# Rotary embedding on one core: 2 MB transfers, and the adds of ten of 32 tiles on TensorE

## The chip, the cores and the metric

The kernel runs on one core of a Trainium2 chip. The metric is the device time of one execution in microseconds (us); lower is better. The profile of the changed kernel shows the timelines of five engines: TensorE (PE, 160 instructions, and PEld for its 160 weight loads), VectorE (DVE, 61), ScalarE (ACT, 43), GpSimd (POOL, 62) and SyncE (SP), which issues the loads (17). The stores are issued by ScalarE, and the page counts 16 DMA engines that carry the transfers. Waits of one engine for another stand in the trace as semaphore instructions (25 on the line of DVE's adds). The span in a profile is 1.7 to 2.1 us shorter than the device time of the same execution.

## The reference

The input x has 8 × 2048 × 8 × 64 elements of fp32 (33.5 MB), and the output is as large. Each half row of 32 is combined with the other half:

```python
def reference(x, cos, sin):
    x1 = x[..., : x.shape[-1] // 2]
    x2 = x[..., x.shape[-1] // 2 :]
    cos = cos[None, :, None, :]
    sin = sin[None, :, None, :]
    out1 = x1 * cos - x2 * sin
    out2 = x1 * sin + x2 * cos
    return np.concatenate([out1, out2], axis=-1)
```

So every output element is one product with cos, one product with plus or minus sin of the other half, and one add.

## The kernel before

The data are cut into 32 tiles of 128 partitions × 2048 elements, 1 MB each. For a tile, GpSimd makes the two sine products (1024 elements per partition each) into a buffer t2, DVE makes the cosine product into t1 and then adds t1 and t2 into the tile itself, which is stored from there. The buffers: there are three of t2, one of t1 (in PSUM), and twenty tiles of x.

```python
    t1_pool = ctx.enter_context(tc.tile_pool(name="t1p", bufs=1, space=bass.MemoryType.PSUM))
    xpool = ctx.enter_context(tc.tile_pool(name="xpool", bufs=20))
    t2_pool = ctx.enter_context(tc.tile_pool(name="t2p", bufs=3))
    # ... tables of cos and sin ...
    for i, (b, l) in enumerate(tiles):
        xt = xpool.tile([P, FREE], f32, tag="xt", name=f"xt{i}")
        nc.sync.dma_start(out=xt, in_=xv[b, :, l * FREE : (l + 1) * FREE])
        xts.append(xt)
    # ...
    for i, (b, l) in enumerate(tiles):
        xt = xts[i]
        t1 = t1_pool.tile([P, FREE], f32, tag="t1")
        t2 = t2_pool.tile([P, FREE], f32, tag="t2")
        for u in range(2):
            # dst, src: views of the two halves of t2 and of xt (cut)
            nc.gpsimd.tensor_mul(out=dst..., in0=src..., in1=rep(ssin[...], H))      # L73
        nc.vector.tensor_mul(out=t1..., in0=xt..., in1=rep(cos_ps[...], 2 * H))     # L78
        nc.vector.tensor_add(out=xt, in0=t1, in1=t2)                                # L83
        nc.scalar.dma_start(out=ov[b, :, l * FREE : (l + 1) * FREE], in_=xt)
```

## Time and profile before

| | before |
|---|---|
| device time, median of 3 | 168.17 us |
| span of the profiled run | 166.6 us |
| DVE busy | 148.2 us |
| GpSimd busy | 146.3 us |
| bytes moved | 67.65 MB |

These lines are from the page of the kernel before: the span, the busy times, and the 40 slices of the span, in which a digit is a busy share in tenths (9 is 90% or more).

```profile
DVE 148.2 (89%) x67; POOL 146.3 (88%) x68
...
DVE  0169999999999999999999999999999999999980
POOL 0299999999999999999999999999999999998000
DMA  5999999999999999999999999999999999999656
...
DVE 89%; DMA 5%; issue 2%; DVEq 0%; ACTq 0%
...
L73 POOL TENSOR_TENSOR t<-xt,ssin 128x1024 f32<-128x1024 f32 x64 | 146.1, 2341 | 6.8 <-DVE ssin L58 6.8
L83 DVE TENSOR_TENSOR xt<-t,t 128x2048 f32<-128x2048 f32 x32 | 73.3, 2291 | 3.3
L78 DVE TENSOR_TENSOR t<-xt,cos_ps 128x2048 f32<-128x2048 f32 x32 | 73.5, 2296 | 1.1
```

The line that begins "DVE 89%" is the chain of waits, followed back from the last instruction: nearly all of it is DVE. The three groups below it end with "idle before, releaser". GpSimd's 64 products were idle only for the 6.8 us of the start, so GpSimd never waits for a buffer; DVE's adds and products lose next to nothing. Three resources are full together: DVE, GpSimd and, until the last three slices, the DMA engines. Relief of one of them alone can win little: 67.65 MB at the 427 GB/s of the middle (next view) are 158 us without start and end (here and below, GB/s count loads and stores together).

In windows of the span (start and end, then its length, busy time of each engine with the number of instructions, the granted TensorE clock, the DMA share and GB/s), before reads:

```profile
40.00:80.00 40.00, 38.79 (x18) 40.00 (x18) 1.00 1.01 427
130.00:167.00 37.00, 30.88 (x14) 23.36 (x11) 1.00 0.87 364
```

The first busy column is DVE, the second GpSimd. In the middle stage both work nearly all the time *at the same time*.

### The profile page before, as it was taken

Reading aid. Unit: us, or ns where it says so; the run is one execution under the profiler, and the core shown is the slowest. Engines: PE = TensorE matmul, PEld = TensorE weight load, DVE = VectorE, ACT = ScalarE, POOL = GpSimd, SP = SyncE. Lnnn points to the kernel's source line nnn. Section 1 sums busy time; section 2 is a strip of 40 time slices with the busy share of each in tenths; the row PEclk is TensorE's granted clock in tenths of the full one; section 3 lists DMA queues with packets and bytes.
Section 4 is the critical chain, followed back from the end, with each engine's and each line's share of the span. In section 5 each row is a group of like instructions: output and inputs, shape, how many; then the busy total and the mean of one; then the engine's idle time right before and its main releaser. Section 6 shows DMA issues by size and latency. Waiting matters only on the chain.

```text
span 166.6 us, 381 instructions
## 1 busy us (share of the span) xinstructions
DVE 148.2 (89%) x67; POOL 146.3 (88%) x68
## 2 busy tenths in 40 slices
DVE  0169999999999999999999999999999999999980
POOL 0299999999999999999999999999999999998000
DMA  5999999999999999999999999999999999999656
GB/s 167 424 428 421 374 431 423 433 427 425 431 421 431 429 427 427 425 433 419 433 425 423 433 419 433 423 433 427 425 431 421 431 427 427 429 423 433 285 220 252
DMA packets 9506, 67.65 MB, mean 406 GB/s; under 512 B 1056, under 2 KB 1056, under 8 KB 1312
## 3 DMA queue, kind: packets, MB, share of 16 engines
q10 hardware_dynamic: 4896, 34.08, 48.6%
q1 hardware_dynamic: 4608, 33.56, 48.3%
q14 instruction: 2, 0.02, 0.0%
HBM read 34.08 MB, written 33.55 MB: 406 GB/s over the span
## 4 chain that ended last, share of the span: by engine, by line
DVE 89%; DMA 5%; issue 2%; DVEq 0%; ACTq 0%
DVE t L78 44%; DVE xt L83 44%; DMA cos_sb<-in_cos_dram 5%; DVE cos_ps L60 0%; DVEq L83 0%; ACTq L48 0%
## 5 line engine op out<-in xcount | busy, mean ns | idle before, releaser
L73 POOL TENSOR_TENSOR t<-xt,ssin 128x1024 f32<-128x1024 f32 x64 | 146.1, 2341 | 6.8 <-DVE ssin L58 6.8
L83 DVE TENSOR_TENSOR xt<-t,t 128x2048 f32<-128x2048 f32 x32 | 73.3, 2291 | 3.3
L78 DVE TENSOR_TENSOR t<-xt,cos_ps 128x2048 f32<-128x2048 f32 x32 | 73.5, 2296 | 1.1
L58 DVE TENSOR_SCALAR ssin<-sin_sb 128x512 f32<-128x512 f32 x1 | 0.4, 426 | 6.7 <-DMA sin_sb<-in_sin_dram 6.7
L60 DVE COPY cos_ps<-cos_sb 128x512 f32<-128x512 f32 x1 | 0.7, 694 | 2.4 <-DMA cos_sb<-in_cos_dram 2.4
L59 DVE COPY ssin<-sin_sb 128x512 f32<-128x512 f32 x1 | 0.4, 419 | 0.0
L99 POOL MEMSET const-float32-0.0<- 128x1 f32 x1 | 0.1, 98 | 0.2 <-issue 0.2
L99 POOL MEMSET const-bfloat16-1.0<- 128x1 bf16 x1 | 0.1, 101 | 0.0
L99 POOL MEMSET const-uint8-127<- 128x1 uint8 x1 | 0.1, 101 | 0.0
L99 POOL MEMSET const-float32-1.0<- 128x1 f32 x1 | 0.1, 98 | 0.0
## 6 DMA issues: line engine op xcount, KB each, us to landing
xt<-in_x_dram SPq DMA_DIRECT2D x32, 1024.0 KB, 20.6
out_dram<-xt ACTq DMA_DIRECT2D x32, 1024.0 KB, 10.7
sin_sb<-in_sin_dram ACTq DMA_DIRECT2D x1, 256.0 KB, 6.0
cos_sb<-in_cos_dram ACTq DMA_DIRECT2D x1, 256.0 KB, 8.7
```

The costliest lines, as they stand in the source:

```text
L58: nc.vector.tensor_scalar_mul(ssin[:, :, 0, :], sin_sb, -1.0)
L59: nc.vector.tensor_copy(ssin[:, :, 1, :], sin_sb)
L60: nc.vector.tensor_copy(cos_ps, cos_sb)
L73: nc.gpsimd.tensor_mul(out=dst.rearrange("p (r h) d -> p r h d", h=H), in0=src.rearrange("p (r h) d -> p r h d", h=H), in1=rep(ssin[:, l * ...
L78: nc.vector.tensor_mul(out=t1.rearrange("p (r k d) -> p r k d", r=SL, d=Dh), in0=xt.rearrange("p (r k d) -> p r k d", r=SL, d=Dh), in1=rep ...
L83: nc.vector.tensor_add(out=xt, in0=t1, in1=t2)
L99: nc = _bacc.Bacc("TRN2", target_bir_lowering=False, num_devices=1)
```

## The change

The intent is to relieve the two busy engines and to make transfers cheaper. Tiles are loaded and stored in pairs of 2 MB, with rows of 16 KB instead of 8 KB. Twenty-two tiles (kind A) are computed as before. In six tiles (kind B), TensorE adds: a matmul with the identity as weights puts t1 into PSUM, a second one accumulates t2 on top, and ScalarE copies the sum to the tile. In four tiles (kind C), DVE makes both products, GpSimd is left out, and TensorE and ScalarE do the rest. For kinds B and C, t1 lies in SBUF in buffers of its own (t1s, two of them), and t2 gives up one of its three buffers. In the listing, line 118 is the GpSimd product, 123 DVE's cosine product, 129 DVE's add, 111 DVE's sine product of kind C, 134 and 135 the matmuls of kind B with the copy in 136, and 143, 144 and 147 the same of kind C.

```diff
-    xpool = ctx.enter_context(tc.tile_pool(name="xpool", bufs=20))
-    t2_pool = ctx.enter_context(tc.tile_pool(name="t2p", bufs=3))
+    o_pool = ctx.enter_context(tc.tile_pool(name="op", bufs=2, space=PSUM))
+    xpool = ctx.enter_context(tc.tile_pool(name="xpool", bufs=10))
+    t1s_pool = ctx.enter_context(tc.tile_pool(name="t1s", bufs=2))
+    t2_pool = ctx.enter_context(tc.tile_pool(name="t2p", bufs=2))
 ...
+        xt = xpool.tile([P, PAIR], f32, tag="xt", name=f"xt{i}")
+        for lo, n in [(0, FREE), (FREE, FREE)] if i == 0 else [(0, PAIR)]:
+            nc.sync.dma_start(out=xt[:, lo : lo + n], in_=xv[b, :, l * PAIR + lo : l * PAIR + lo + n])
 ...
+    kinds = {3: "C", 11: "C", 18: "C", 24: "C", 6: "B", 9: "B", 14: "B", 16: "B", 21: "B", 27: "B"}
 ...
+        if kind == "A":
+            t1 = t1_pool.tile([P, FREE], f32, tag="t1")
+        else:
+            t1 = t1s_pool.tile([P, FREE], f32, tag="t1s")
 ...
+        if kind == "C":
+            nc.vector.tensor_mul(out=t2..., in0=xk, in1=rep(sin_ps[...], 2 * H))
+        else:
+            # the two GpSimd products, as before
 ...
-        nc.vector.tensor_add(out=xt, in0=t1, in1=t2)
+        if kind == "A":
+            nc.vector.tensor_add(out=xt, in0=t1, in1=t2)
+        elif kind == "B":
+            for j in range(FREE // C):
+                o = o_pool.tile([P, C], f32, tag="o")
+                cs = slice(j * C, (j + 1) * C)
+                nc.tensor.matmul(o, eye, t1[:, cs], start=True, stop=False)
+                nc.tensor.matmul(o, eye, t2[:, cs], start=False, stop=True)
+                nc.scalar.copy(xt[:, cs], o)
+        else:
+            # the same with the halves of t2 swapped, and -identity for one of them
 ...
+        elif half:
+            nc.scalar.dma_start(out=ov[b, :, base : base + PAIR], in_=pt)
```

The last pair is stored as two halves of 1 MB, the first pair loaded as two halves. In SBUF the pools of x are equal before and after (20 × 1 MB, 10 × 2 MB).

More of the change, by code (lines that the diff above doesn't have):

```diff
@@ L20 @@
     f32 = mybir.dt.float32
+    PSUM = bass.MemoryType.PSUM
     B, S, H, D = x.shape
@@ L28 @@
     SL = 4
-    n_blk = R // SL
     FREE = SL * HD
+    PAIR = 2 * FREE
+    n_pair = R // (2 * SL)
+    C = 512
     xv = x.rearrange("b (q r) h d -> b q (r h d)", q=P)
@@ L37 @@
     const_pool = ctx.enter_context(tc.tile_pool(name="const", bufs=1))
-    cps_pool = ctx.enter_context(tc.tile_pool(name="cps", bufs=1, space=bass.MemoryType.PSUM))
-    t1_pool = ctx.enter_context(tc.tile_pool(name="t1p", bufs=1, space=bass.MemoryType.PSUM))
-    xpool = ctx.enter_context(tc.tile_pool(name="xpool", bufs=20))
-    t2_pool = ctx.enter_context(tc.tile_pool(name="t2p", bufs=3))
+    tab_pool = ctx.enter_context(tc.tile_pool(name="tab", bufs=1, space=PSUM))
+    t1_pool = ctx.enter_context(tc.tile_pool(name="t1p", bufs=1, space=PSUM))
+    o_pool = ctx.enter_context(tc.tile_pool(name="op", bufs=2, space=PSUM))
+    xpool = ctx.enter_context(tc.tile_pool(name="xpool", bufs=10))
+    t1s_pool = ctx.enter_context(tc.tile_pool(name="t1s", bufs=2))
+    t2_pool = ctx.enter_context(tc.tile_pool(name="t2p", bufs=2))
     cos_sb = const_pool.tile([P, R, Dh], f32, tag="cb")
@@ L45 @@
     ssin = const_pool.tile([P, R, 2, Dh], f32, tag="ss")
-    cos_ps = cps_pool.tile([P, R, Dh], f32, tag="cp")
+    eye = const_pool.tile([P, P], f32, tag="eye")
+    neye = const_pool.tile([P, P], f32, tag="neye")
+    cos_ps = tab_pool.tile([P, R, Dh], f32, tag="cp")
+    sin_ps = tab_pool.tile([P, R, Dh], f32, tag="sp")
     nc.scalar.dma_start(out=sin_sb, in_=sin_src)
     nc.scalar.dma_start(out=cos_sb, in_=cos_src)
-    tiles = [(b, l) for l in range(n_blk) for b in range(B)]
+    pairs = [(b, l) for l in range(n_pair) for b in range(B)]
     xts = []
-    for i, (b, l) in enumerate(tiles):
-        xt = xpool.tile([P, FREE], f32, tag="xt", name=f"xt{i}")
-        nc.sync.dma_start(out=xt, in_=xv[b, :, l * FREE : (l + 1) * FREE])
-        xts.append(xt)
+    for i, (b, l) in enumerate(pairs):
+        xt = xpool.tile([P, PAIR], f32, tag="xt", name=f"xt{i}")
+        for lo, n in [(0, FREE), (FREE, FREE)] if i == 0 else [(0, PAIR)]:
+            nc.sync.dma_start(
+                out=xt[:, lo : lo + n],
+                in_=xv[b, :, l * PAIR + lo : l * PAIR + lo + n],
+            )
+        xts.append(xt)
+    nc.gpsimd.memset(eye, 0.0)
+    nc.gpsimd.affine_select(
+        out=eye,
+        in_=eye,
+        compare_op=mybir.AluOpType.not_equal,
+        fill=1.0,
+        base=0,
+        pattern=[[-1, P]],
+        channel_multiplier=1,
+    )
     nc.vector.tensor_scalar_mul(ssin[:, :, 0, :], sin_sb, -1.0)
@@ L60 @@
     nc.vector.tensor_copy(cos_ps, cos_sb)
+    nc.scalar.copy(sin_ps, sin_sb)
+    nc.scalar.mul(neye, eye, -1.0)
     def rep(a, n):
         return dataclasses.replace(a, ap=[a.ap[0][:], a.ap[1][:], [0, n], a.ap[-1][:]])
-    for i, (b, l) in enumerate(tiles):
-        xt = xts[i]
-        t1 = t1_pool.tile([P, FREE], f32, tag="t1")
-        t2 = t2_pool.tile([P, FREE], f32, tag="t2")
-        for u in range(2):
-            dst = t2.rearrange("p (rh u d) -> p rh u d", u=2, d=Dh)[:, :, u, :]
-            src = xt.rearrange("p (rh u d) -> p rh u d", u=2, d=Dh)[:, :, 1 - u, :]
-            nc.gpsimd.tensor_mul(
-                out=dst.rearrange("p (r h) d -> p r h d", h=H),
-                in0=src.rearrange("p (r h) d -> p r h d", h=H),
-                in1=rep(ssin[:, l * SL : (l + 1) * SL, u, :], H),
-            )
+    kinds = {3: "C", 11: "C", 18: "C", 24: "C", 6: "B", 9: "B", 14: "B", 16: "B", 21: "B", 27: "B"}
@@ new lines @@
+    n_tiles = 2 * len(pairs)
+    for i in range(n_tiles):
+        b, l = pairs[i // 2]
+        pt = xts[i // 2]
+        half = i % 2
+        xt = pt[:, half * FREE : (half + 1) * FREE]
+        r0 = (2 * l + half) * SL
+        kind = kinds.get(i, "A")
+        xk = xt.rearrange("p (r k d) -> p r k d", r=SL, d=Dh)
+        xu = xt.rearrange("p (g u d) -> p g u d", u=2, d=Dh)
+        t2 = t2_pool.tile([P, FREE], f32, tag="t2")
+        t2u = t2.rearrange("p (g u d) -> p g u d", u=2, d=Dh)
+        if kind == "A":
+            t1 = t1_pool.tile([P, FREE], f32, tag="t1")
+        else:
+            t1 = t1s_pool.tile([P, FREE], f32, tag="t1s")
+        t1u = t1.rearrange("p (g u d) -> p g u d", u=2, d=Dh)
+        if kind == "C":
+            nc.vector.tensor_mul(
+                out=t2.rearrange("p (r k d) -> p r k d", r=SL, d=Dh),
+                in0=xk,
+                in1=rep(sin_ps[:, r0 : r0 + SL, :], 2 * H),
+            )
+        else:
+            for u in range(2):
+                nc.gpsimd.tensor_mul(
+                    out=t2u[:, :, u, :].rearrange("p (r h) d -> p r h d", h=H),
+                    in0=xu[:, :, 1 - u, :].rearrange("p (r h) d -> p r h d", h=H),
+                    in1=rep(ssin[:, r0 : r0 + SL, u, :], H),
+                )
@@ L78 @@
         nc.vector.tensor_mul(
             out=t1.rearrange("p (r k d) -> p r k d", r=SL, d=Dh),
-            in0=xt.rearrange("p (r k d) -> p r k d", r=SL, d=Dh),
-            in1=rep(cos_ps[:, l * SL : (l + 1) * SL, :], 2 * H),
-        )
-        nc.vector.tensor_add(out=xt, in0=t1, in1=t2)
-        nc.scalar.dma_start(out=ov[b, :, l * FREE : (l + 1) * FREE], in_=xt)
+            in0=xk,
+            in1=rep(cos_ps[:, r0 : r0 + SL, :], 2 * H),
+        )
+        if kind == "A":
[8 more added lines that the diff above has]
+        else:
+            G = C // Dh
+            for u in range(2):
+                for j in range(FREE // 2 // C):
+                    o = o_pool.tile([P, C], f32, tag="o")
+                    gs = slice(j * G, (j + 1) * G)
+                    nc.tensor.matmul(o, eye, t1u[:, gs, u, :], start=True, stop=False)
+                    nc.tensor.matmul(
+                        o, eye if u else neye, t2u[:, gs, 1 - u, :], start=False, stop=True
+                    )
+                    nc.scalar.copy(xu[:, gs, u, :], o.rearrange("p (g d) -> p g d", d=Dh))
@@ L88 @@
+        base = l * PAIR
+        if i == n_tiles - 2:
+            nc.scalar.dma_start(out=ov[b, :, base : base + FREE], in_=xt)
+        elif i == n_tiles - 1:
+            nc.scalar.dma_start(out=ov[b, :, base + FREE : base + PAIR], in_=xt)
+        elif half:
+            nc.scalar.dma_start(out=ov[b, :, base : base + PAIR], in_=pt)
 _INS = ['x', 'cos', 'sin']
```

## The prediction

It was written before the changed kernel had run. The program had been built, so its order of instructions and its semaphore waits were known.

> **What bounds the kernel now.** Two things, nearly in balance. The chain of waits is DVE for 89% of the span (line 78 44%, line 83 44%); the groups give 2296 and 2291 ns per instruction, so one 1 MB tile costs DVE 4.73 us (starts in the timeline: 10.64, 15.37, 20.09). GpSimd runs beside it: two products of 2341 ns, 4.65 us per tile, never waiting after the first 6.8 us. The slices show DMA at 99% and 419 to 433 GB/s until about 155 us; 67.65 MB at 427 GB/s is 158 us. Only the last 12 us are paced by DVE alone.
>
> **What the change does, per engine.** DVE: 22 tiles keep product and add, six (B) only a product, four (C) two products: 22×4.73 + 6×2.36 + 4×4.73 = 137 us instead of 151. GpSimd: 28×4.65 = 130 us instead of 149. Transfers: an 8 KB packet took 309 ns and a 2 KB packet 84 ns, so about 9 ns a packet are fixed; 16 KB rows would save some 1.5%, 2 us of transfer time. If everything overlapped, the span would be about 160 us. I do not believe it.
>
> **What it adds: lost overlap.** The product buffers t2 go from three to two, and a B or C tile keeps one while TensorE adds. I followed the built program's order and semaphore waits. The remaining buffer then serves one A tile after another, so GpSimd waits for the DVE add (2.3 us) before each next tile, and DVE waits for GpSimd's 4.65 us: about 7.1 us per tile instead of 4.73. The program has 13 GpSimd products that wait like this for the add just before (first: tile 5 waits for the add of tile 4; likewise 8, 9, 13, 14, 16, 20, 21, 23, 26, 27, 29, 30), each about 2.45 us: 32 us. Tile 4 waits about 5 us for the add of tile 2, because DVE does a C product first. At least two tiles (12 and 19) wait for TensorE to release a buffer.
>
> **TensorE.** No trace of it yet. [...]
>
> **Sum.** GpSimd: start 7.3 + 130 + 32 + 5 + about 9 = 183 to 185 us; then the last add (2.4) and the last stores, where ScalarE's queue puts one 2 MB and two 1 MB stores behind the last adds (about 8 us): span about 196 us. Before, the device time was 1.6 us above the span. Prediction: 198 us, 8 in 10 between 190 and 210. Faster by over 2%: 0.03; within 2%: 0.03; slower by over 2%: 0.94.
>
> **What the profile would show if right.** Waits: GpSimd idle for DVE line 129 about 13 times and over 30 us, DVE idle for GpSimd line 118 over 30 us. Windows: DMA share well under 1 after the first 40 us, mean about 345 GB/s. Instruction durations on DVE and GpSimd unchanged. The chain: GpSimd and DVE alternate, GpSimd the larger share. If wrong: DMA at 99% to the end, and GpSimd without gaps.
>
> **What would make it wrong.** [...] GpSimd or DVE running faster when alone would lower it. If the waits did not bind, transfers would end it near 162.

The sum came to 183 to 185 us for GpSimd's end, 196 us of span and 198 us of device time. The sum's term "about 9", GpSimd's waits for TensorE, rested on the author's estimate of a matmul's duration. The run then measured these waits at 8.4 us.

## The result

The changed kernel takes 195.91 us (median of 4 runs, 194.23 to 196.30) against 168.18 us (168.14 to 168.40) of the kernel before on the same chip. The ratio is 1.163, with a 95% interval from 1.156 to 1.170: slower by 16%. Ratios here and below are the mean time of one kernel's fast runs over the mean of the other's of the same rounds, so they are not quite the ratio of the medians.

The page after, with the lines that answer to those of before:

```profile
span 194.3 us, 670 instructions
...
PE 91.8 (47%) x160; PEld 36.2 (19%) x160; DVE 132.9 (68%) x61; ACT 25.2 (13%) x43; POOL 129.7 (67%) x62
...
DVE  0199999981996394994581979906999960955940
POOL 1599345998659636859598459595972689559900
PEclk9999999996955599855796999658859965885555
DMA  6999999999999999999999999990069950008596
...
L118 POOL TENSOR_TENSOR t<-xt,ssin 128x1024 f32<-128x1024 f32 x56 | 129.0, 2332 | 53.8 <-DVE xt L129 39.4
L129 DVE TENSOR_TENSOR xt<-t,t 128x2048 f32<-128x2048 f32 x22 | 50.4, 2292 | 43.8 <-POOL t L118 43.4
L123 DVE TENSOR_TENSOR t<-xt,cos_ps 128x2048 f32<-128x2048 f32 x32 | 72.4, 2290 | 0.6
L135 PE MATMUL o<-t,eye 128*128 128x512 f32 x48 | 33.7, 797 | 23.5 <-POOL t L118 23.5
```

The work did go down: DVE is busy 15.3 us less and GpSimd 16.6 us less. A single product or add takes what it took (2332 and 2292 ns beside 2341 and 2291). What is new stands at the ends of the first two groups. GpSimd's products now wait 39.4 us for DVE's adds, and DVE's adds wait 43.4 us for GpSimd's products. Two engines that wait for each other no longer overlap.

The timeline of GpSimd after shows it (start, duration, instruction, how many in a row, and in brackets the idle time before with its releaser):

```profile
26.72 4.61 POOL L118 TENSOR_TENSOR t<-xt,ssin 128x1024 f32<-128x1024 f32 x2 [5.77 <-DVE xt L129]
...
50.10 4.61 POOL L118 TENSOR_TENSOR t<-xt,ssin 128x1024 f32<-128x1024 f32 x2 [2.40 <-DVE xt L129]
57.12 9.20 POOL L118 TENSOR_TENSOR t<-xt,ssin 128x1024 f32<-128x1024 f32 x4 [2.40 <-DVE xt L129]
71.16 4.63 POOL L118 TENSOR_TENSOR t<-xt,ssin 128x1024 f32<-128x1024 f32 x2 [4.85 <-issue]
78.19 4.62 POOL L118 TENSOR_TENSOR t<-xt,ssin 128x1024 f32<-128x1024 f32 x2 [2.40 <-DVE xt L129]
85.21 9.21 POOL L118 TENSOR_TENSOR t<-xt,ssin 128x1024 f32<-128x1024 f32 x4 [2.40 <-DVE xt L129]
```

Two products of GpSimd are one tile. Tile after tile starts 7.02 us apart (50.10, 57.12; 78.19, 85.21) where before it was 4.7 us: 4.62 us of products, then 2.40 us in which GpSimd stands still while DVE adds. Twelve of its gaps are exactly 2.40 us. The other side of the alternation is in DVE's timeline of the same stretch:

```profile
54.74 2.29 DVE L129 TENSOR_TENSOR xt<-t,t 128x2048 f32<-128x2048 f32 x1 [0.20 <-POOL t L118]
57.07 4.49 DVE L123 TENSOR_TENSOR t<-xt,cos_ps 128x2048 f32<-128x2048 f32 x2
66.34 2.29 DVE L129 TENSOR_TENSOR xt<-t,t 128x2048 f32<-128x2048 f32 x1 [4.79 <-POOL t L118]
```

GpSimd's product at 57.12 begins when the add of 54.74 has ended (57.03). The add at 66.34 in turn starts when GpSimd's four products (57.12 + 9.20 = 66.32) are done. Why must they alternate, with two buffers of t2? The built program assigns t2's two buffers to the tiles in their order. Tile 3 (kind C) and tile 6 (kind B) take one of them, and it stays taken while TensorE works on it; the tiles of kind A around them (4, 5, 7, 8) all get the other. By the program's semaphores, one buffer is not filled by GpSimd while DVE reads it (hence the start at 57.12 after the end at 57.03). This assignment is read off the built program; the trace shows no buffer numbers, but its waits agree.

The assignment is fixed when the program is built, and it costs waits even when TensorE holds nothing. If the products, adds and matmuls of the trace are put to their tiles in the program's order, five of GpSimd's 14 waits for adds (before tiles 9, 14, 21, 27 and 30, 12.0 us of 39.4) came while no TensorE tile held a t2 buffer. The wait before 57.12 is one of them: TensorE's last matmul of tile 6 had ended at 50.27. The last is here; TensorE's last matmul of all ends at 170.12, and GpSimd still waits for an add until 174.94:

```profile
169.53 0.59 PE L135 MATMUL o<-t,eye 128*128 128x512 f32 x1
...
174.94 9.16 POOL L118 TENSOR_TENSOR t<-xt,ssin 128x1024 f32<-128x1024 f32 x4 [2.40 <-DVE xt L129]
```

How long TensorE holds a buffer is in its timeline (start, duration; each row is one matmul of the program, which the trace shows as two PE instructions):

```profile
63.64 1.91 PE L134 MATMUL o<-t,eye 128*128 128x512 f32 x2
65.34 1.92 PE L135 MATMUL o<-t,eye 128*128 128x512 f32 x2
67.05 1.39 PE L134 MATMUL o<-t,eye 128*128 128x512 f32 x2
...
69.14 1.02 PE L134 MATMUL o<-t,eye 128*128 128x512 f32 x2
70.00 1.02 PE L135 MATMUL o<-t,eye 128*128 128x512 f32 x2
```

Starts are 1.70 us apart at first and 0.86 us later. The granted clock was 0.50 from 62 to 67 us and 1.00 from 68 to 72 us; here the change comes some 5 us into the burst, which began at 61.77 us. What makes the clock change was not shown. The row PEclk of the page above shows the two as 5s and 9s. It says nothing of the first burst, though: the trace's records of the clock begin only at 33.66 us, and the row reads 9 before them, where the starts from 28.98 us on are 1.84 and 1.71 us apart. The gap of 4.85 us before GpSimd's product at 71.16 is labelled "issue", which means that the profile found no releaser. TensorE's last matmul of tile 9 ends at 71.02, and the built program makes tile 12's product wait for it; the same holds for 3.58 us at 109.63, after a matmul that ended at 109.49.

The whole difference can be added up on GpSimd. Its last product ended at 153.4 us before (119.09 + 34.27, the last row of its timeline) and ends at 184.1 us after (174.94 + 9.16): 30.7 us later. It worked 17.1 us less (146.1 to 129.0), waited 39.4 us for adds and 8.4 us for TensorE: −17.1 + 39.4 + 8.4 = 30.7. From its end to the end of the span there were 13.2 us before and 10.2 after, so the span grew by 27.7 us.

Last, the DMA engines, in windows after (here the busy columns are PE, PEld, DVE, ACT and POOL):

```profile
40.00:80.00 40.00, 25.55 (x45) 9.96 (x44) 27.50 (x13) 5.85 (x10) 27.94 (x13) 0.79 1.01 431
130.00:195.00 65.00, 25.59 (x45) 10.01 (x43) 40.98 (x18) 6.83 (x12) 39.66 (x18) 0.68 0.47 200
```

DMA is full in a stage in which DVE and GpSimd work only 70% of the time. The loads run ahead into the ten buffers. The last six of them had to wait for a store to free a buffer (SyncE waited 70.7 us, six times), but enough transfers were on their way to keep the engines full; the last load has landed by about 127 us, and the engines are full until about 130 us. Then only stores are left, and they come as slowly as the compute makes them: 0.47 of the DMA engines for 65 us. A reader of the DMA row alone would have called the first 130 us bound by DMA.

### The profile page after: what moved, and what is told of

It reads as the page before. It is cut to its first block, busy times and chain, and to the rows that moved or that the text cites. A ratio compares the mean times of both kernels' runs of the same rounds, so it can differ in the third digit from the quotient of the medians.

```text
span 194.3 us, 670 instructions
## 1 busy us (share of the span) xinstructions
PE 91.8 (47%) x160; PEld 36.2 (19%) x160; DVE 132.9 (68%) x61; ACT 25.2 (13%) x43; POOL 129.7 (67%) x62
## 5 line engine op out<-in xcount | busy, mean ns | idle before, releaser
L118 POOL TENSOR_TENSOR t<-xt,ssin 128x1024 f32<-128x1024 f32 x56 | 129.0, 2332 | 53.8 <-DVE xt L129 39.4
L129 DVE TENSOR_TENSOR xt<-t,t 128x2048 f32<-128x2048 f32 x22 | 50.4, 2292 | 43.8 <-POOL t L118 43.4
L123 DVE TENSOR_TENSOR t<-xt,cos_ps 128x2048 f32<-128x2048 f32 x32 | 72.4, 2290 | 0.6
L135 PE MATMUL o<-t,eye 128*128 128x512 f32 x48 | 33.7, 797 | 23.5 <-POOL t L118 23.5
L134 PE MATMUL o<-t,eye 128*128 128x512 f32 x48 | 32.4, 767 | 18.9 <-DVE t L123 10.6
L143 PE MATMUL o<-t,eye 128*128 128x512 f32 x32 | 19.0, 679 | 35.5 <-DVE t L123 29.0
L136 ACT COPY xt<-o 128x512 f32<-128x512 f32 x24 | 13.8, 586 | 92.1 <-PE o L135 75.2
L135 PEld LDWEIGHTS o<-t,eye 128*128 128x128 f32 x48 | 11.2, 246 | 42.2 <-POOL t L118 29.9
L134 PEld LDWEIGHTS o<-t,eye 128*128 128x128 f32 x48 | 11.5, 251 | 37.1 <-issue 27.0
L147 ACT COPY xt<-o 128x512 f32<-128x512 f32 x16 | 9.3, 586 | 53.7 <-PE o L144 43.2
L143 PEld LDWEIGHTS o<-t,eye 128*128 128x128 f32 x32 | 6.8, 219 | 43.8 <-issue 36.5
L144 PE MATMUL o<-t,neye 128*128 128x512 f32 x16 | 9.7, 696 | 0.5 <-DVE t L111 0.5
L111 DVE TENSOR_TENSOR t<-xt,sin_ps 128x2048 f32<-128x2048 f32 x4 | 9.1, 2287 | 0.3
L144 PE MATMUL o<-t,eye 128*128 128x512 f32 x16 | 8.2, 593 | 0.0
L144 PEld LDWEIGHTS o<-t,neye 128*128 128x128 f32 x16 | 3.6, 232 | 6.1 <-issue 3.7
L144 PEld LDWEIGHTS o<-t,eye 128*128 128x128 f32 x16 | 3.0, 190 | 3.8 <-issue 3.8
L83 ACT COPY sin_ps<-sin_sb 128x512 f32<-128x512 f32 x1 | 0.6, 590 | 3.7 <-DMA sin_sb<-in_sin_dram 3.7
```

The source lines that it names most:

```text
L83: nc.scalar.copy(sin_ps, sin_sb)
L111: nc.vector.tensor_mul(out=t2.rearrange("p (r k d) -> p r k d", r=SL, d=Dh), in0=xk, in1=rep(sin_ps[:, r0 : r0 + SL, :], 2 * H),)
L118: nc.gpsimd.tensor_mul(out=t2u[:, :, u, :].rearrange("p (r h) d -> p r h d", h=H), in0=xu[:, :, 1 - u, :].rearrange("p (r h) d -> p r h d" ...
L123: nc.vector.tensor_mul(out=t1.rearrange("p (r k d) -> p r k d", r=SL, d=Dh), in0=xk, in1=rep(cos_ps[:, r0 : r0 + SL, :], 2 * H),)
L134: nc.tensor.matmul(o, eye, t1[:, cs], start=True, stop=False)
L135: nc.tensor.matmul(o, eye, t2[:, cs], start=False, stop=True)
```

## The experiments

The theory was that the number of free t2 buffers does it: with two, and one held by TensorE, GpSimd and DVE take turns. The rivals put the loss elsewhere: on the path over TensorE and ScalarE as such (part of its matmuls at a granted clock of 0.50, its copies in one queue with the stores), or on the large transfers with their fewer and larger buffers. All listed runs gave correct results within the comparison's tolerance. A kernel with one run: its time is to be read to a few microseconds only; all the other times below are medians of four fast runs.

### One t1s buffer given to t2, same memory

```diff
-    t1s_pool = ... bufs=2
-    t2_pool = ... bufs=2
+    t1s_pool = ... bufs=1
+    t2_pool = ... bufs=3
```

> One 8 KB buffer moves from the TensorE product pool (t1s 2 to 1) to t2 (2 to 3); SBUF use, tiles, transfers and TensorE work stay. Theory (buffers): TensorE may hold one t2 buffer, two stay for GpSimd and DVE, so they overlap again: 162 to 167 us, GpSimd waits for the add (line 129) fall from 39 us to under 10. Rival 1 (TensorE and ScalarE themselves are too slow, 92 us of PE at half clock): nothing of theirs got faster, so within 4 us of 196. Rival 2 (the 2 MB transfers with ten big buffers free buffers too late): also near 196.

Measured: 164.91 us (164.66 to 165.02), ratio to before 0.981 (0.979 to 0.982). Thirty-one microseconds (195.91 to 164.91, beside 168.18 and 168.15 of before) went by moving one buffer, and the kernel is now a little faster than before. From its page:

```profile
DMA  5999999999999999999999999999999999999993
...
L118 POOL TENSOR_TENSOR t<-xt,ssin 128x1024 f32<-128x1024 f32 x56 | 128.9, 2344 | 20.3 <-DVE xt L129 13.8
```

The waits of GpSimd for adds fell from 39.4 to 13.8 us (expected: under 10, so a miss in size), and DMA is full until the last slice. TensorE and ScalarE did the same matmuls and copies (83.4 us busy, beside 91.8), and the transfers are the same 2 MB. So neither of these as such can have cost the 28 us. (The expectation's "92 us of PE at half clock" overstates it: the mean granted clock of the changed kernel was 0.789. Of its 159 steps from one matmul instruction to the next, 46 took 0.64 to 1.07 us and 102 took 0.43 to 0.57 us. Of the latter, 94 took 0.43 us, all at a granted clock of 1.00; the steps of 0.85 us start at 0.50 wherever the clock is on record.)

### The control: one t1s buffer fewer, t2 left at two

```diff
-    t1s_pool = ... bufs=2
+    t1s_pool = ... bufs=1
```

> Control for the run before: t1s 2 to 1 alone, t2 stays at two. Theory (buffers): one t2 buffer is left beside the held one, as in the changed kernel, so 194 to 206 us. If fewer t1s buffers were what helped, it would be near 165.

Measured: 201.31 us in one run, inside what the theory expected. GpSimd waited 44.8 us for adds, 15 times:

```profile
POOL t L118 <- DVE xt L129: 44.8, 15, 5.8
```

So the missing t1s buffer alone wins nothing, and the first experiment's gain needs the third t2 buffer. The next one shows that the third t2 buffer alone is not enough either.

### Three and four t2 buffers with both t1s buffers

The memory comes from xpool, which goes from ten pairs to nine.

```diff
-    xpool = ... bufs=10
-    t2_pool = ... bufs=2
+    xpool = ... bufs=9
+    t2_pool = ... bufs=3      # and, in a second kernel, bufs=4
```

> t2 2 to 3 with t1s left at 2, paid for by x buffers 10 to 9. A third t2 buffer but TensorE tiles may hold two at once. Theory (buffers, free ones count): still only one free in stretches where two TensorE tiles are in flight, so only part comes back: 178 to 194 us. Simple form of the theory (a third buffer is enough): 163 to 168.

> t2 2 to 4, t1s 2, x buffers 9: SBUF use as in the changed kernel. Theory (buffers): two held, two free: 163 to 168 us. Rival 2 (x buffers too few): worse than 196, as there is one fewer. Rival 1 (TensorE too slow): near 196.

Measured: 191.81 us with three (one run), 164.91 us with four (164.69 to 165.08; ratio 0.981, 0.979 to 0.982). Both fell where the theory had put them: with both t1s buffers the program can have two tiles under way on TensorE, each of which holds a t2, and by that count three buffers less two are again one. The waits of the kernel with three, and with four (engine and line, whom it waited for, us in total, times, longest):

```profile
ACT xt L147 <- DVE xt L129: 50.1, 3, 25.1
...
PEld o L134 <- ACT xt L147: 47.4, 3, 23.8
...
POOL t L118 <- DVE xt L129: 39.0, 11, 7.4
```

```profile
POOL t L118 <- DVE xt L129: 9.8, 4, 4.6
```

The first two lines say why TensorE held its tiles so long in the kernel with three: it waited up to 23.8 us for ScalarE to empty its PSUM tile, and ScalarE's copies came up to 25.1 us late because in the program's order a store, which waited for an add of DVE, stands before them. So the slow consumer at the end of the path lengthened the hold here; with four buffers it did no harm (33.6 us of the same ScalarE wait, and 164.91 us).

The trace does not show the count itself. Put to their tiles as above, two TensorE tiles held t2 at once for only about 20 us in the kernel with three buffers and both t1s, and for about 31 us in the first experiment, where the loss is gone. And in nine of the eleven waits of GpSimd in the kernel with three (28.7 us of 39.0), one of the three buffers was in use by no tile. So the count that fits the times, buffers less those that can be held at once, is one that the built program's order of buffers and waits goes by, and not what is free on the chip at the moment. That the single t1s buffer of the first experiment helps because it makes DVE wait before a second tile can be given to TensorE (6.5 us in all, two waits) is argued, not shown.

### No TensorE tile at all, t2 still at two

```diff
-    kinds = {3: "C", 11: "C", ...}
+    kinds = {}
```

> The changed kernel with no TensorE tile: 2 MB transfers, two t2 buffers, all 32 adds on DVE. Theory (a buffer held by TensorE is what serializes): with no holder two buffers are enough, GpSimd never waits over 1 us for an add, and DVE bounds it as before: 167.5 to 169 us. If two t2 buffers alone were the cause, it would be 190 or more. It also measures the 2 MB transfers alone: within 0.5% of before, since DVE bounds it.

Measured: 168.31 us, ratio 1.001 (0.999 to 1.004), the time of before. GpSimd's one wait of note is at the start:

```profile
POOL t L118 <- DVE ssin L80: 5.9, 1, 5.9
```

Two t2 buffers were enough where nothing but DVE holds them, so the loss is neither in the two buffers alone nor in the 2 MB transfers; it takes both the two buffers and tiles that go to TensorE. The run also shows that 2 MB transfers by themselves won nothing while DVE set the pace (ratio 1.001).

### A shorter hold: matmuls of bf16

Matmuls read only the upper 16 bits of each fp32 number as bf16. That drops precision on purpose, and is no version to use.

```diff
+    def hi(a):
+        return a.bitcast(bf16).rearrange("p (n two) -> p n two", two=2)[:, :, 1]
 ...
-                nc.tensor.matmul(o, eye, t1[:, cs], start=True, stop=False)
+                nc.tensor.matmul(o, hi(eye), hi(t1[:, cs]), start=True, stop=False)
```

> Wrong result on purpose (low half of each value dropped): the matmuls read the upper 16 bits of eye, t1 and t2 as bf16, [...] two t2 buffers and two t1s as in the changed kernel. Theory (held buffer): a shorter hold gives much of the loss back, as the order of buffers can alternate more: 168 to 180 us. If the count of buffers mattered and not the time they are held, it would stay near 195.

Measured: 169.41 us in one run. In the first burst (28.55 to 31.49 us) matmuls start about 0.42 us apart, and each is one PE instruction of the trace instead of two; in the first burst of the changed kernel, the first starts were 1.84 and 1.71 us apart. The clock of this burst was not read; the run's mean is 0.626. TensorE is busy 37.2 us instead of 91.8, and GpSimd's waits for adds fell to 22.6 us, seven times. This fits the theory, but it isn't a clean test of the hold time: in this program the buffers were also assigned differently to the tiles (they alternate more), so the part of each is not separated.

### Transfers of 1 MB, one direction or both

These three start from the first experiment (t2 three, t1s one). In the first, loads and stores are both of 1 MB; in the others only the stores, or only the loads.

```diff
-        for lo, n in [(0, FREE), (FREE, FREE)] if i == 0 else [(0, PAIR)]:
+        for lo, n in [(0, FREE), (FREE, FREE)]:                      # loads of 1 MB
 ...
-        base = l * PAIR
-        ... (stores of whole pairs)
+        base = l * PAIR + half * FREE                                # stores of 1 MB
+        nc.scalar.dma_start(out=ov[b, :, base : base + FREE], in_=xt)
```

> The mended kernel (t2 three, t1s one) with 1 MB loads and stores with 8 KB rows again. Theory (that one is bound by transfers): packets of 8192 B at 309 ns instead of 16384 B at 611 ns lower the rate from about 432 to 427 GB/s: 1.5 to 2.5 us slower than the 2 MB form, 166 to 167.5 us. If the 2 MB rows did nothing there, 164.9.

> The mended kernel (t2 three, t1s one) with 2 MB loads and 1 MB stores. Packet theory: half of the packets are small, 0.7 to 1.3 us over 164.9: 165.5 to 166.3 us. Prefetch theory: large loads keep the prefetch deep, so about the same 165 to 166.5 us.

> The mended kernel with 1 MB loads and 2 MB stores. Packet theory: the same as the run with 1 MB stores, 165.5 to 166.3 us. Prefetch theory: small loads are what hurts, 167 to 170 us, with GpSimd or DVE waiting for data.

Measured: 168.65 us with both at 1 MB (ratio to before 1.002, 0.998 to 1.006), 167.89 us with 2 MB loads and 1 MB stores (0.998, 0.994 to 1.001), 169.03 us with 1 MB loads and 2 MB stores (1.006, 1.002 to 1.009). All three lose the gain. The first run missed what was expected of it and was slower; the second lies outside what either theory expected; the third fell where a theory of loads that lag behind had put it, but GpSimd and DVE show no wait for data there, which that theory also expected. The size of the packets can't explain it alone. From the traces (medians, before and after), a packet of 2048 B took 84 ns, one of 8192 B took 309 ns and one of 16384 B took 611 ns, 305.5 ns per 8 KB; that is 1.1%, or an estimated 1.7 us of the 158 us, not 3.7 us. New waits appeared in the kernel with both at 1 MB (two lines of its waits, then two of its timelines):

```profile
ACT xt L136 <- DMA xt<-in_x_dram: 17.5, 2, 13.2
...
DVE t L123 <- PE o L134: 10.7, 2, 8.7
...
94.69 2.28 DVE L129 TENSOR_TENSOR xt<-t,t 128x2048 f32<-128x2048 f32 x1
...
97.05 22.96 POOL L118 TENSOR_TENSOR t<-xt,ssin 128x1024 f32<-128x1024 f32 x10 [10.85 <-DMA out_dram<-xt]
```

ScalarE's copies have no load to wait for by themselves (DVE's product has read it before). Before the copy that waited 13.2 us, two stores stand in ScalarE's queue, and each was issued just after a load had landed (landings at 76.52 and 81.42, stores at 76.59 and 81.49). The transfers of each kernel share eight semaphores in the trace (at most eight were under way at once in the kernel before, seven in the changed one), and each of these stores uses that of the load it waited for. So TensorE was late, and DVE waited up to 8.7 us for it. GpSimd's wait of 10.85 us carries the label of a store, but its product began at 97.05, right after DVE's add had ended (94.69 + 2.28 = 96.97), as after the other adds: it waited for DVE. In the first experiment the same wait was 6.6 us and DVE's longest wait for TensorE 4.5 us. These some 4.2 us more are near the 3.7 us lost; no run isolates them.

The two mixed kernels show something else. Their DMA queues between 40 and 60 us of the span (queue, packets, MB, share of the engines; q1 carries the loads, q10 the stores), first with 2 MB loads and 1 MB stores, then the other way:

```profile
q1 hardware_dynamic: 393, 5.65, 66.0%
q10 hardware_dynamic: 399, 2.88, 34.0%
```

```profile
q10 hardware_dynamic: 380, 5.70, 66.6%
q1 hardware_dynamic: 383, 2.85, 33.7%
```

A packet of the trace is one row: the changed kernel has 30 transfers of 2 MB with 128 rows each, and its trace 3841 packets of 16384 B. (96 of the 792 packets of the first window and 67 of the 763 of the second are under 512 B.) Packets are about equal in number (393 and 399, 380 and 383), so the bytes are divided as the row sizes are: the side with the larger rows had two thirds of them (5.65 of 8.53 MB, 5.70 of 8.55 MB). How the DMA engines choose between the queues was not shown. With small load rows, the last load landed at about 143 us instead of 137 in the first experiment (GpSimd's waits for adds rose to 18.5 us, DVE's for TensorE to 14.9 us). With small store rows SyncE waited 93.1 us in all, instead of 53.4, for stores before it could issue loads, though the last load landed earlier, at about 126 us. Which of these waits costs the last 3 to 4 us of each was not separated.

### Fewer TensorE tiles, spread out, and the same with 1 MB

```diff
-    xpool = ... bufs=10
-    t2_pool = ... bufs=2
-    kinds = {3: "C", 11: "C", 18: "C", 24: "C", 6: "B", 9: "B", 14: "B", 16: "B", 21: "B", 27: "B"}
+    xpool = ... bufs=9
+    t2_pool = ... bufs=4
+    kinds = {3: "C", 8: "B", 13: "C", 18: "B", 22: "B", 27: "B"}
```

> Four t2 buffers, x buffers nine, six TensorE tiles instead of ten (C at 3 and 13, B at 8, 18, 22, 27), placed further apart. Theory (transfers bound the mended forms): four tiles fewer for TensorE do not change the time: 164.3 to 165.3 us, as the two mended forms before. If compute still bounded those, it would be over 1 us off 164.9 to either side.

> The fastest form so far (six TensorE tiles, four t2 buffers) with 1 MB loads and stores. Packet theory (only the rate counts, 309 ns per 8 KB against 611 per 16 KB): 1.5 to 2.5 us over 164.6, so 166 to 167.2 us, with no engine waiting for a load. Prefetch theory (eight transfers in flight hold half the bytes, so loads come late, as seen in the mended kernel with 1 MB): more, 167 to 169.5 us, and waits of GpSimd or DVE for data.

Measured: 164.61 us (164.43 to 164.65), ratio 0.979 (0.976 to 0.982), for the six tiles with 2 MB; 165.93 us (165.54 to 166.52), ratio 0.986 (0.984 to 0.989), for the same with loads and stores of 1 MB. The first has the lowest time and beats both given kernels, though its interval reaches across 2% and overlaps those of the two kernels at 164.91 us, which ran on another chip. The second lies just below what the packet theory expected (166 to 167.2). From its page and its windows:

```profile
DMA  5999999999999999999999999999999999999994
...
L118 POOL TENSOR_TENSOR t<-xt,ssin 128x1024 f32<-128x1024 f32 x60 | 137.6, 2349 | 6.9 <-DVE ssin L80 5.6
```

```profile
80.00:120.00 40.00, 18.92 (x32) 7.63 (x32) 39.20 (x18) 4.69 (x8) 40.00 (x18) 0.74 1.01 431
```

GpSimd waits 5.6 us at the start and only 1.3 us, once, for an add, so DVE and GpSimd overlap nearly all the time, and DMA is full to the last slice, while DVE and GpSimd do nothing in the last 13 us (windows from 150 us on). Here the transfers are the limit. The row size is worth 1.3 us between the two kernels, near the 1.7 us estimated from the packets; since GpSimd also waited 9.4 us, once, for TensorE in the kernel with 1 MB, and ScalarE's copies 45.8 us behind loads, this is agreement and no proof. Four tiles fewer on TensorE than in the first experiment cost nothing, since DVE (137.5 us busy) and GpSimd (138.3 us) stay below the transfers' time.

## Why the prediction was right

The time (198.0, measured 195.91, inside 190 to 210) and the direction were right, and so was the mechanism. The prediction had followed the built program's order and waits, so it counted them as they are. By its steps:

- **What bounds before.** Right. DVE and GpSimd were in balance, with DMA full beside them; the run without TensorE tiles reproduces it at 168.31 us. (The page shows 9s, that is 90% or more, where the prediction says 99%; the windows give a share of 1.01.)
- **GpSimd waits for the add just before.** Right. The prediction had 13 waits of 2.45 us and one of 5 us: 37 us. Measured were 14 waits and 39.4 us: twelve of 2.40 us, one of 5.77 us (tile 4) and one of 4.83 us (tile 26), which had been counted as 2.45. Its one sentence of reason, that TensorE keeps a buffer, covers nine of these waits; in the other five (12.0 us) TensorE held none, and the wait comes from the program's fixed order.
- **DVE waits for GpSimd over 30 us.** Right: 43.4 us.
- **Two waits for TensorE, about 9 us.** Right: 4.85 and 3.58 us, together 8.4 us. The author's estimate of a matmul behind these 9 us is cut, as no trace stood behind it; measured are starts 1.70 us apart at a granted clock of 0.50 and 0.86 us at 1.00, and 9.4 us for the first burst (28.98 to 38.40 us).
- **GpSimd ends at 183 to 185 us, about 8 us after the last add.** Right: 184.1 us, and 7.7 us from the last add (184.30 + 2.29) to the end. These parts add up to 193.4 to 195.4 us of span (measured 194.3); the prediction took 196, and that rounding is most of its 2 us too much.
- **DVE's work 137 us.** A little too large: 132.9 us busy. The estimate used 2.36 us from start to start, which counts the gaps between instructions (2.29 us long); two products in a row came 2.2 us apart. DVE was not what paced the kernel, so this did not count.
- **16 KB rows save 1.5%.** Too large: 1.1% per byte. It did not count either.
- **"DMA share well under 1 after the first 40 us".** Wrong. The share was 1.00 to 1.01 until some 130 us, and 0.47 from there on. The mean of 348 GB/s was right (about 345 predicted), but it is no steady rate: the loads that ran ahead kept the engines full until there was nothing left to load. The step that failed was to take a low mean for a low share in every stage.
- **The chain.** It does alternate, with GpSimd 23% and DVE 9% of the span, but the trace's chain begins only at 101.46 us, so it is weak evidence.

Shown by runs is that too few t2 buffers for the tiles that go to TensorE cost the time: same memory, one buffer moved, and 195.91 us became 164.91 us; with no TensorE tile two buffers suffice; with both t1s buffers three do not and four do. Left open are how much is due to buffers that TensorE really holds and how much to the order in which the built program assigns them (another assignment of the same two buffers, or stores on another queue than ScalarE's to shorten the hold, was not tried), the part of matmul speed in the kernel with bf16 matmuls (169.41 us with two buffers of each), and how far the waits found above explain why ten TensorE tiles lose 3.7 us with transfers of 1 MB (164.91 to 168.65) where six lose 1.3 us.

## What to carry to other kernels

When work moves to another engine, count for each buffer how many its new reader can hold at once: what overlaps a producer with a consumer is the buffers that remain, and in these runs it took at least two (164.91 us where two remained by that count, 191.81 and 201.31 us where one did). Count them in the built program, where the assignment is fixed, and not by what looks free in the trace. A longer path that holds a buffer can turn relief of the busy engines into alternation, and one buffer of 1 MB moved between pools was worth 31 us here, with the same memory. A DMA row full of nines may only be loads that run ahead, as here, where the share was 1.00 to 1.01 until some 130 us and 0.47 from there on; look at what is left when they have ended.
